# Splitting 24 weight pieces in the second half of the projection phase, and alternating two products in the tail

## The chip, the cores and the metric

One core of one Trainium2 chip. The metric is the device time of one execution in microseconds (us), the median of several runs.

## What is computed

One layer of a hybrid encoder on 2048 prompt and 32 sample tokens, model width 1024, all in float32. `z = rmsnorm(x) @ W_in` gives q, k, v, an attention gate, the inputs of a short convolution, and two merge gates. What matters here is what follows:

```python
y_a = (attn * silu(gate_a)) @ w_attn_out          # 512 -> 1024
y_c = (b_gate * conv * silu(gate_c)) @ w_conv_out # 512 -> 1024
r = x + (sigmoid(merge_a) * y_a + sigmoid(merge_c) * y_c) @ w_o
r = r + sigmoid(r @ w_ple_gate) * (p @ w_ple_proj)
```

## The kernel before

**Arithmetic.** A float32 product is made of three TensorE passes: each operand is split into a high half, rounded to the fast format fp32r, and a low half, the rest; the passes are high x high, high x low, low x high. ScalarE makes the high half with a copy, VectorE the low half with a subtraction (`split`, L228). A *piece*, or quad, is a weight tile of 128 x 512 numbers, 256 KB. The three large matrices W_in, W_o (`UO`) and W_pg (`UPG`) go through Strassen-Winograd: seven products instead of eight, for which four sums of weight pieces are needed (`make_sums` L353 for W_in, `quad_sums` L381 for W_o and W_pg: sc, a21, a11 and a12, four additions on VectorE). The sums are stored in DRAM by DMAs that GpSimd issues.

**Phases.** Tokens are worked on in two halves. The first phase (0 to about 870 us in the trace) is the projection with W_in: `steps` (L244 to L288), first the 21 groups of the first half `(0, g, p)`, then those of the second half `(1, g, p)`, whose products p = 2, 3, 4 are split once more into sets (`run_set`, L755; the letters A to G are its small products; GpSimd adds the weights for p = 3 and 4 in `load_set`, L448). A scheduler puts the instructions of this phase in order on each engine; a pool of 15 temporaries (`tp`, tag `t`, L50) serves the evictions, and from group 7 on `second_half` (L571), which loads rows of x, normalises them, combines them and stores them. The rest (yB, pp, yA, and the Strassen products with W_o and W_pg, called b0-50, b0-58, b1-50, b1-58 for the two halves) is a list of units, `plan` (L307 to L318), which `run_units` (L2020) issues in order; a planner in the kernel keeps a clock of its own (`now`, `busy`, `fin`), and decides by it when evictions, loads (`next_loads`, L1961) and the 17 attention tiles (`attention`, L1380; the start times stand in `begin`, L2070 to L2079) are issued between the products. All engines execute their queues in order.

**The 24 pieces.** The four sums of each of four columns of W_o make 16 pieces, the upper half of the yA/yB weights (`wa`) makes 8. They are wanted split in the second phase, so the kernel splits them in the first: at steps `(0, g, 6)` and `(0, g, 7)` of the first half, the loads at the first and the rest one step later (`sums_at`, L1234 to L1237). `quad_sums(UO, n)` runs at g = 1, 3, 5, 7, `piece_split(n)` (L394) at g = 2, 4, ... 16, `quad_sums(UPG, n)`, which stores unsplit sums, at g = 9, 11, 13, 15. The quads lie in a pool of their own (`zpool`, five buffers, L1232). `store_split` (L375) splits and stores both halves, 512 KB. In the second phase such a piece comes back as one load of 512 KB, straight into the split weights (`stored`, L399; L1998 to L2009); all other weights are loaded raw, 256 KB, and split there by ScalarE and VectorE (`split_w`, L1947).

**The planner's wire.** `Engine.call` (L141) reckons when a DMA has landed. In the second phase `wire[0]` is None after `restart()` (L211), so a transfer counts 5.2 us, one that accumulates 6.6 us, however many are under way.

**The tail of the first half.** `plan` has the 28 products of b0-58 (W_pg), then the eight units yA of block 2, then the first four products of b1-50.

## Time and profile before

| | us |
|---|---|
| median of 3 runs | 1543.53 |
| lowest and highest run | 1542.6, 1543.53 |
| the profiled execution | 1542.36 |
| its span, first to last instruction | 1540.6 |
| TensorE (PE) busy | 1501.9 |
| VectorE (DVE) busy | 1196.2 |
| ScalarE (ACT) busy | 795.0 |
| GpSimd (POOL) busy | 388.5 |

The profile is of one execution. PE is TensorE's matmul, PEld its loading of weights, SPq SyncE's queue of DMA issues. L158 is the line in the planner's helper from which nearly all instructions of the second phase come, so there one goes by tiles. In rows of stages the last three numbers are the granted clock of TensorE (1.00 is full), the busy share of the 16 DMA engines, and GB/s. "Busy" counts only instructions that compute; the time before an instruction is idle time, and the arrow names what ended it.

### The profile page before, as it was taken

The numbers are of one execution on the slowest core, as the hardware profiler recorded it, in microseconds if no ns is written. First come the engines' busy times: TensorE is split into PE (matmuls) and PEld (weight loads), VectorE is DVE, ScalarE is ACT, GpSimd is POOL, SyncE is SP. The second block draws the span as 40 slices with busy tenths as digits, with TensorE's granted clock in tenths as the row PEclk, the third lists the DMA queues.
The fourth block names the chain that finished last, engine by engine and source line by source line (L and its number), as shares of the span: only waits on it lengthen the run. The fifth ranks groups of instructions, "written<-read, shape, count | busy, mean of one in ns | idle before, by whom it ended". The sixth has DMA issues, their size and how long they took to land.

```text
span 1540.6 us, 27844 instructions
## 1 busy us (share of the span) xinstructions
PE 1501.9 (97%) x9553; PEld 1354.6 (88%) x9553; DVE 1196.2 (78%) x2290; ACT 795.0 (52%) x1893; POOL 388.5 (25%) x566
## 2 busy tenths in 40 slices
PE   9999999989999999999999999999999999899998
PEld 7778888768889999999999999998888788799998
DVE  7896887777568877799966778867898899367777
ACT  8364355234457654443445646685755668132453
POOL 2133332233221332333311221102313112110201
PEclk9999999999999999999999999999999999999999
DMA  9469798899887964334556785779888759998959
GB/s 362 161 224 358 263 326 270 294 334 348 287 281 249 319 218 155 123 118 133 158 182 195 249 257 184 216 251 255 252 238 244 193 153 262 325 300 267 278 147 286
DMA packets 202941, 374.14 MB, mean 243 GB/s; under 512 B 24368, under 2 KB 57712, under 8 KB 202800
## 3 DMA queue, kind: packets, MB, share of 16 engines
q1 hardware_dynamic: 158160, 258.30, 51.7%
q0 software_dynamic: 34992, 96.24, 21.2%
q10 hardware_dynamic: 9648, 17.83, 3.1%
q8 instruction: 75, 1.23, 0.3%
q14 instruction: 66, 0.54, 0.1%
HBM read 246.53 MB, written 125.85 MB: 242 GB/s over the span
## 4 chain that ended last, share of the span: by engine, by line
PE 72%; DMA 11%; DVE 7%; issue 6%; ACT 3%; POOL 1%; SPq 0%; POOLq 0%; DVEq 0%; ACTq 0%
PE b L158 13%; PE a L638 7%; PE a L643 7%; PE a L640 7%; PE yB L158 6%; PE la L776 5%; PE yA L158 4%; PE c L638 3%; PE c L640 3%; PE c L643 3%; DMA wr<-in_wu 3%; PE lc L776 2%; DVE c L158 2%; PE O L158 2%; PE S L158 1%
## 5 line engine op out<-in xcount | busy, mean ns | idle before, releaser
L158 PE MATMUL b<-xb_h,w 128*128 128x264 f32 (+1 forms) x1344 | 311.5, 324 | 0.0
L158 PEld LDWEIGHTS b<-xb_h,w 128*128 128x128 f32 x1344 | 223.6, 189 | 19.3 <-DVE c L158 1.4
L638 PE MATMUL a<-x_h,w 128*128 128x264 f32 (+1 forms) x744 | 228.7, 321 | 7.5 <-ACT u L832 6.1
L640 PE MATMUL a<-x_l,w 128*128 128x264 f32 (+1 forms) x744 | 228.5, 320 | 0.0
L158 PE MATMUL b<-xb_l,w 128*128 128x264 f32 (+1 forms) x672 | 218.4, 325 | 2.3 <-DVE xb_l L158 2.3
L643 PE MATMUL a<-x_h,w 128*128 128x264 f32 (+1 forms) x744 | 202.2, 321 | 0.0
L229 ACT CAST w<-wr 128x512 fp32r<-128x512 f32 (+1 forms) x180 | 110.0, 618 | 112.6 <-PE c L643 32.4
L230 DVE TENSOR_TENSOR w<-wr,w 128x512 fp32r<-128x512 f32 (+1 forms) x180 | 135.7, 764 | 39.7 <-ACT w L229 39.5
L638 PEld LDWEIGHTS a<-x_h,w 128*128 128x128 f32 x744 | 140.4, 189 | 19.2 <-ACT u L832 7.0
L640 PEld LDWEIGHTS a<-x_l,w 128*128 128x128 f32 x744 | 140.4, 189 | 10.7
L158 PEld LDWEIGHTS b<-xb_l,w 128*128 128x128 f32 x672 | 126.9, 189 | 12.4 <-DVE xb_l L158 3.8
L643 PEld LDWEIGHTS a<-x_h,w 128*128 128x128 f32 x744 | 125.3, 188 | 10.8 <-DVE w L230 0.2
L776 PE MATMUL la<-x_h,w 128*128 128x264 f32 x516 | 111.6, 285 | 1.0 <-ACT w L229 0.7
L158 ACT CAST w<-wr 128x512 fp32r<-128x512 f32 x104 | 63.7, 620 | 92.9 <-PE b L158 50.5
L638 PE MATMUL c<-x_h,w 128*128 128x512 f32 (+1 forms) x336 | 110.9, 340 | 0.0
L640 PE MATMUL c<-x_l,w 128*128 128x512 f32 (+1 forms) x336 | 110.8, 340 | 0.0
L643 PE MATMUL c<-x_h,w 128*128 128x512 f32 (+1 forms) x336 | 100.3, 340 | 0.0
L158 PE MATMUL yA<-ac_h,w 128*128 128x264 f32 (+1 forms) x384 | 93.6, 330 | 6.0 <-DMA w<-wa 5.9
L229 ACT CAST w<-a 128x512 fp32r<-128x512 f32 x82 | 49.0, 620 | 85.6 <-DVE a L360 48.8
L158 PE MATMUL yB<-ycs_h,w 128*128 128x264 f32 (+1 forms) x384 | 90.4, 325 | 0.0
L837 DVE SCALAR_TENSOR_TENSOR u<-u,c 128x264 f32<-128x264 f32 (+1 forms) x125 | 59.4, 506 | 39.8 <-ACT u L832 28.5
L776 PEld LDWEIGHTS la<-x_h,w 128*128 128x128 f32 x516 | 86.9, 188 | 1.6 <-ACT w L229 1.0
(446 smaller groups left out, 3861.9 us busy)
## 6 DMA issues: line engine op xcount, KB each, us to landing
wr<-in_wu SPq DMA_DIRECT2D x145, 256.0 KB, 4.5
a<-in_wu SPq DMA_DIRECT2D x116, 256.0 KB, 5.6
wr<-ws SPq DMA_DIRECT2D x74, 256.0 KB, 3.7
w<-wa SPq DMA_DIRECT2D x32, 512.0 KB, 5.7
w<-qs SPq DMA_DIRECT2D x32, 512.0 KB, 5.4
ws<-a POOLq DMA_DIRECT2D x63, 256.0 KB, 3.7
wr<-qs SPq DMA_DIRECT2D x32, 256.0 KB, 4.6
qs<-a POOLq DMA_DIRECT2D x24, 256.0 KB, 6.5
```

Source lines behind the costliest of these rows:

```text
L158: return f(**kw)
L229: nc.scalar.copy(out=hi, in_=src)
L230: nc.vector.tensor_tensor(out=lo, in0=src, in1=hi.bitcast(F32), op=sub)
L638: nc.tensor.matmul(out=ps[:, :cn], lhsT=w[:, 0, k], rhs=x[0][:, c0:c0 + cn], start=first and k == 0, stop=False, skip_group_check=True)
L640: nc.tensor.matmul(out=ps[:, :cn], lhsT=w[:, 0, k], rhs=x[1][:, c0:c0 + cn], start=False, stop=False, skip_group_check=True)
L643: nc.tensor.matmul(out=ps[:, :cn], lhsT=w[:, 1, k], rhs=x[0][:, c0:c0 + cn], start=False, stop=k == 3, skip_group_check=True)
L776: nc.tensor.matmul(out=ps[:, :m], lhsT=w[:, a, k], rhs=r[:, cols], start=q in "ABG" and j == 0 and e == 0, stop=j == 1 and e == 2, skip_gr ...
L837: nc.vector.scalar_tensor_tensor(out=t[:, c0:c0 + cn], in0=t[:, c0:c0 + cn], scalar=-1.0, in1=ps[:, :cn], op0=mul, op1=sub)
```

## The change

1. **Sums and splits apart.** `quad_sums` now only adds and stores the four sums unsplit, for W_o and W_pg alike, all eight calls in groups 1 to 8 of the first half, loads and additions in one step. Its quads and sum lie in the shared pool of 15 temporaries.
2. **Splits in the second half.** The 24 pieces are split by `half_steps`, in four stages with a distance: load (lag 0), ScalarE's copy (lag 9), VectorE's subtraction (lag 11), two stores (lag 12). The pieces follow one another at an even pitch over the steps from (1, 3, 1) on, by step lengths that the code assumes; `in_turn` fixes the place of each in its engine's queue. Their tiles use the pool of five buffers.
3. **Raw weights for the last yA.** `stored` gives split pieces for yA of blocks 0 and 1 only; blocks 2 and 3 load 256 KB and split.
4. **Alternation.** The eight yA units of block 2 alternate with the last eight products of b0-58.
5. **The planner.** `wire[0]` starts at 0.0 in the second phase, so DMAs queue for a shared wire (360 KB per us, 190 for accumulation). Attention tiles 8 to 16 begin 10 us earlier and a little closer together, and the gated attention rows of blocks 2 and 3 may be split earlier (`ac_open`).

```diff
+                        rate = 390e3 if not LATE["V"] else 360e3 if kw.get("accum_op") is None else 190e3
+                        wire[0] = end = max(end + 1.7, wire[0]) + o.shape[0] * size(o) * 4 / rate
...
-    plan += first[:4] + pps[12:] + mixed(1, first[4:8]) + first[8:] + products_of(0, UPG)
-    plan += [("yA", 2, n) for n in NA[2]] + second[:4] + mixed(3, second[4:8]) + second[8:] + products_of(1, UPG)
+    plan += first[:4] + pps[12:] + mixed(1, first[4:8]) + first[8:]
+    tail, ys = products_of(0, UPG), [("yA", 2, n) for n in NA[2]]
+    plan += tail[:-8] + [v for i in range(8) for v in (ys[i], tail[i - 8])]
+    plan += second[:4] + mixed(3, second[4:8]) + second[8:] + products_of(1, UPG)
...
     def quad_sums(x, n):
-        t = {name: quad_load(f"{name}_{x}_{n}", x + u, e)
-             for name, u, e in (("a11", n, 0), ("a21", n + 4, 0), ("a22", n + 4, 1), ("a12", n, 1))}
-        yield
-        t["sc"] = zp.tile([P, 4 * P], F32, tag="z", name=f"sc_{x}_{n}")
+        t = {}
+        for name, u, e in (("a11", n, 0), ("a21", n + 4, 0), ("a22", n + 4, 1), ("a12", n, 1)):
+            t[name] = tmp(f"{name}_{x}_{n}")[:, :512]
+            nc.sync.dma_start(out=t[name].rearrange("p (a b) -> p a b", a=4), in_=wu[x + u, :, 4 * e:4 * e + 4, :])
+        t["sc"] = tmp(f"sc_{x}_{n}")[:, :512]
...
         for p, o in ((7, "sc"), (5, "a21"), (6, "a11"), (3, "a12")):
-            if x == UO:
-                store_split(quad_sum[x, n][:, WS[p]], t[o], f"{p}_{x}_{n}")
+            nc.gpsimd.dma_start(out=quad_sum[x, n][:, WS[p]], in_=t[o])
+
+    def in_turn(engine):
+        return tc.issue_after(next(i for i in reversed(nc.cur_bb.bb.instructions) if i.engine == engine))
+
+    def half_steps(key, dst):
+        name = "_".join(map(str, key))
+        t = zp.tile([P, 4 * P], F32, tag="z", name=f"z{name}")
+        with in_turn(nc.sync.engine):
+            if key[0] == "wa":
+                nc.sync.dma_start(out=t.rearrange("p (a b) -> p a b", a=4), in_=wu[UY + key[1], :, 0:4, :])
             else:
-                nc.gpsimd.dma_start(out=quad_sum[x, n][:, WS[p], 0], in_=t[o])
+                nc.sync.dma_start(out=t, in_=quad_sum[UO, key[1]][:, WS[key[2]]])
+        yield
+        h = zp.tile([P, 4 * P], F32R, tag="z", name=f"h{name}")
+        with in_turn(nc.scalar.engine):
+            nc.scalar.copy(out=h, in_=t)
+        yield
+        with in_turn(nc.vector.engine):
+            nc.vector.tensor_tensor(out=t.bitcast(F32R), in0=t, in1=h.bitcast(F32), op=sub)
         yield
+        with in_turn(nc.gpsimd.engine):
+            nc.gpsimd.dma_start(out=dst[:, 0], in_=h.bitcast(F32))
+            nc.gpsimd.dma_start(out=dst[:, 1], in_=t)
+        yield

     def stored(key):
-        if key[0] == "q" and key[3] == 0:
-            return wa_split[key[2] - UY]
+        if key[0] == "q" and key[3] == 0 and key[1] < 2:
+            return halves["wa", key[2] - UY]
...
-    sums_at = {(0, 1 + 2 * n, 6): quad_sums(UO, n) for n in range(4)}
-    sums_at.update({(0, 9 + 2 * n, 6): quad_sums(UPG, n) for n in range(4)})
-    sums_at.update({(0, 2 + 2 * n, 6): piece_split(n) for n in range(8)})
-    sums_at.update({(0, g, 7): v for (_, g, _), v in sums_at.items()})
+    sums_at = {(0, 1 + 2 * n + e, 6): (x, n) for n in range(4) for e, x in enumerate((UO, UPG))}
+    length = [(2.9 if len(steps[i][0]) == 3 else 0.75) if i >= at_step[1, 3, 1] else 0.0 for i in range(len(steps))]
+    pitch = (sum(length) - 24) / len(halves)
+    half_at = sorted((pitch * j + lag, j, k) for j in range(len(halves)) for k, lag in enumerate((0, 9, 11, 12)))
...
+        while half_at and length[i] and half_at[0][0] <= sum(length[:i]):
+            next(half_gen[half_at.pop(0)[1]])
...
     LATE.update(V=0.08, S=0.1, G=0.25)
+    wire[0] = 0.0
...
-        t = (0, 6)[e] if e < 2 else 11 * e if e < 8 else e1 - 30 + (e2 - e1) * (e - 8) / 9
+        t = (0, 6)[e] if e < 2 else 11 * e if e < 8 else e1 - 40 + 0.96 * (e2 - e1) * (e - 8) / 9
...
-    begin.append((T[f"b0{UPG}_0_2"], lambda: ac_open.add(2)))
-    begin.append((T[f"b1{UO}_0_2"], lambda: ac_open.add(3)))
+    begin.append((T[f"b0{UPG}_0_5"], lambda: ac_open.add(2)))
+    begin.append((T[f"b0{UPG}_1_4"], lambda: ac_open.add(3)))
```

The scheduler of the first phase orders each queue anew. SyncE's queue where the first rows of x for the second half (b00 to b11) are loaded, near 265 us in the trace; wr and a are weights of the current groups, wa_5 a piece of yA, a11_58 to a22_58 quads of W_pg's sums. Before:

```order
L348 DMA wr87_2783<-in_wu 128x512
L372 DMA wa_5_2873<-in_wu 128x512
L372 DMA a11_58_2_3064<-in_wu 128x512
L372 DMA a21_58_2_3066<-in_wu 128x512
L583 DMA b00_0_2801<-in_xT 128x528
L583 DMA b01_0_2804<-in_xT 128x528
L583 DMA b10_0_2807<-in_xT 128x528
L583 DMA b11_0_2810<-in_xT 128x528
L372 DMA a22_58_2_3068<-in_wu 128x512
L348 DMA wr88_2836<-in_wu 128x512
```

The same place on SyncE's queue after the change:

```order
L351 DMA wr87_2743<-in_wu 128x512
L593 DMA b00_0_2761<-in_xT 128x528
L593 DMA b01_0_2764<-in_xT 128x528
L593 DMA b10_0_2767<-in_xT 128x528
L593 DMA b11_0_2770<-in_xT 128x528
L351 DMA wr88_2787<-in_wu 128x512
```

Four piece loads that stood between the two weights wr87 and wr88 have left this place. All quad loads of the eight sums now stand ahead of the last load of group 9's sums, among the loads of groups 3 to 9.

The tail, on SyncE's queue, where the weights of yA of block 2 are loaded (w or wr with a number is a weight, tk2 the merge gate of a yA unit, pp and out_yT belong to products of W_pg). Before:

```order
L158 DMA w445_15986<-wa0_145 128x1024
L158 DMA out_yT<-c21_058_0_7_15128 128x512
L158 DMA out_yT<-c21_058_1_7_15157 128x512
L158 DMA z_at_79<-at3_3_15668 512x1x128
L158 DMA tk2_7_16028<-z_t0_7_107 128x528
L158 DMA w446_16035<-wa1_146 128x1024
L158 DMA tk2_0_16061<-z_t0_0_100 128x528
L158 DMA out_yT<-c21_058_2_7_15204 128x512
L158 DMA w447_16069<-wa2_147 128x1024
L158 DMA tk2_1_16095<-z_t0_1_101 128x528
```

The weights in the tail after the change:

```order
L159 DMA wr445_15924<-in_wu 128x512
L159 DMA out_yT<-c22_058_3_5_15790 128x512
L159 DMA tk2_6_15935<-z_t0_6_106 128x528
L159 DMA wr446_15949<-in_wu 128x512
L159 DMA pp0_2_15973<-z_pp2_86 128x512
L159 DMA wr447_15975<-in_wu 128x512
L159 DMA out_yT<-c12_058_2_6_15235 128x512
L159 DMA tk2_7_15996<-z_t0_7_107 128x528
L159 DMA wr448_15998<-in_wu 128x512
```

Loads of 1024 numbers per row have become loads of 512, and loads of pp for W_pg's products stand between the tk2 loads. On TensorE attention's last product (O_31) stands just ahead of the first yA unit of block 2 in both orders; eight products of b0-58 that stood before it now stand behind it. Its tile 8 (pq2_0) has moved from the fifth unit of yA of block 0 to the second.

More of the change, by code (lines that the diff above doesn't have):

```diff
@@ L155, in call @@
                         o = kw["out"]
-                        wire[0] = end = max(end + 1.7, wire[0]) + o.shape[0] * size(o) * 4 / 390e3
+                        rate = 390e3 if not LATE["V"] else 360e3 if kw.get("accum_op") is None else 190e3
+                        wire[0] = end = max(end + 1.7, wire[0]) + o.shape[0] * size(o) * 4 / rate
                 fin[0] = max(fin[0], end)
@@ L364, in make_sums @@
             nc.gpsimd.dma_start(out=wsum[g][:, i], in_=sums[g][p])
-    quad_sum = {(x, n): dram.tile([P, 4, 1 + (x == UO), 4 * P], F32, tag=f"qs{x}_{n}", name=f"qs{x}_{n}")
-                for x in (UO, UPG) for n in range(4)}
-    wa_split = [dram.tile([P, 2, 4 * P], F32, tag=f"wa{n}", name=f"wa{n}") for n in range(8)]
-    def quad_load(name, u, e):
-        t = zp.tile([P, 4 * P], F32, tag="z", name=name)
-        nc.sync.dma_start(out=t.rearrange("p (a b) -> p a b", a=4), in_=wu[u, :, 4 * e:4 * e + 4, :])
-        return t
-    def store_split(dst, t, name):
-        h = tmp(f"h{name}", F32R)[:, :512]
-        split(h, t.bitcast(F32R), t)
-        nc.gpsimd.dma_start(out=dst[:, 0], in_=h.bitcast(F32))
-        nc.gpsimd.dma_start(out=dst[:, 1], in_=t)
-    def quad_sums(x, n):
-        t = {name: quad_load(f"{name}_{x}_{n}", x + u, e)
-             for name, u, e in (("a11", n, 0), ("a21", n + 4, 0), ("a22", n + 4, 1), ("a12", n, 1))}
-        yield
-        t["sc"] = zp.tile([P, 4 * P], F32, tag="z", name=f"sc_{x}_{n}")
+    quad_sum = {(x, n): dram.tile([P, 4, 4 * P], F32, tag=f"qs{x}_{n}", name=f"qs{x}_{n}") for x in (UO, UPG) for n in range(4)}
+    halves = {("wa", n): dram.tile([P, 2, 4 * P], F32, tag=f"wa{n}", name=f"wa{n}") for n in range(8)}
+    halves.update({("o", n, p): dram.tile([P, 2, 4 * P], F32, tag=f"o{n}_{p}", name=f"o{n}_{p}")
+                   for n in range(4) for p in WS})
+    def quad_sums(x, n):
+        t = {}
[3 more added lines that the diff above has]
+        t["sc"] = tmp(f"sc_{x}_{n}")[:, :512]
         for o, v, w in (("sc", "a11", "a21"), ("a21", "a21", "a22"), ("a11", "a11", "a21"), ("a12", "a12", "a11")):
@@ L388, in quad_sums @@
         for p, o in ((7, "sc"), (5, "a21"), (6, "a11"), (3, "a12")):
[L389 to L395 removed]
+            nc.gpsimd.dma_start(out=quad_sum[x, n][:, WS[p]], in_=t[o])
[7 more added lines that the diff above has]
+                nc.sync.dma_start(out=t.rearrange("p (a b) -> p a b", a=4), in_=wu[UY + key[1], :, 0:4, :])
+            else:
+                nc.sync.dma_start(out=t, in_=quad_sum[UO, key[1]][:, WS[key[2]]])
         yield
[L397 removed]
+        h = zp.tile([P, 4 * P], F32R, tag="z", name=f"h{name}")
[9 more added lines that the diff above has]
+        yield
     def stored(key):
[L400 to L401 removed]
+        if key[0] == "q" and key[3] == 0 and key[1] < 2:
+            return halves["wa", key[2] - UY]
         if key[0] == "B" and key[2] == UO and key[4] in WS:
[L403 removed]
+            return halves["o", key[3], key[4]]
         return None
@@ L1233, in tile_hybrid_stream_step @@
     zp = zpool.__enter__()
-    sums_at = {(0, 1 + 2 * n, 6): quad_sums(UO, n) for n in range(4)}
-    sums_at.update({(0, 9 + 2 * n, 6): quad_sums(UPG, n) for n in range(4)})
-    sums_at.update({(0, 2 + 2 * n, 6): piece_split(n) for n in range(8)})
-    sums_at.update({(0, g, 7): v for (_, g, _), v in sums_at.items()})
+    sums_at = {(0, 1 + 2 * n + e, 6): (x, n) for n in range(4) for e, x in enumerate((UO, UPG))}
+    length = [(2.9 if len(steps[i][0]) == 3 else 0.75) if i >= at_step[1, 3, 1] else 0.0 for i in range(len(steps))]
+    pitch = (sum(length) - 24) / len(halves)
+    half_at = sorted((pitch * j + lag, j, k) for j in range(len(halves)) for k, lag in enumerate((0, 9, 11, 12)))
+    half_gen = [half_steps(*x) for x in halves.items()]
     conv_at = {(1, G - 1, 1): lambda: conv_load(0), (1, G - 1, 6): lambda: (conv_split(0), conv_load(1)),
@@ L1252, in tile_hybrid_stream_step @@
         if todo[0] in sums_at:
-            next(sums_at[todo[0]], None)
+            quad_sums(*sums_at[todo[0]])
+        while half_at and length[i] and half_at[0][0] <= sum(length[:i]):
+            next(half_gen[half_at.pop(0)[1]])
         if i in after:
@@ L1993, in next_loads @@
             else:
-                eY.dma_start(out=t, in_=quad_sum[key[2:4]][:, WS[key[4]], 0].rearrange("p (a b) -> p a b", a=4))
+                eY.dma_start(out=t, in_=quad_sum[key[2:4]][:, WS[key[4]]].rearrange("p (a b) -> p a b", a=4))
             raw_of[i] = t
```

4 lines of the change are left out of this document (removed).

## The prediction

> **What bounds the kernel now.** I read the first page for the share of each engine, then busy time by stage (which stage leaves TensorE idle, and what is full there), then TensorE in order of time for the single stops, and last the queues that end those stops.
>
> From the page: the span and the busy time of each engine.
>
> ```profile
> span 1540.6 us, 27844 instructions
> PE 1501.9 (97%) x9553; PEld 1354.6 (88%) x9553; DVE 1196.2 (78%) x2290; ACT 795.0 (52%) x1893; POOL 388.5 (25%) x566
> ```
>
> TensorE is busy for 1501.9 of 1540.6 us, and the change removes no product. So it can win only the 38.7 us of idle time and what the clock loses behind a stop. Busy time by stage (PE, PEld, DVE, ACT, POOL; then granted clock, DMA share, GB/s) shows where that lies:
>
> ```profile
> 100.00:275.00 175.00, 175.00 (x758) 141.42 (x757) 139.52 (x229) 82.79 (x168) 63.19 (x120) 1.00 0.86 306
> 275.00:345.00 70.00, 58.77 (x233) 46.05 (x232) 51.88 (x83) 20.32 (x36) 23.36 (x44) 0.93 0.89 313
> 642.00:774.00 132.00, 132.00 (x1086) 131.81 (x1085) 122.50 (x244) 56.57 (x123) 50.09 (x71) 1.00 0.44 135
> 1070.00:1310.00 240.00, 234.59 (x1250) 195.96 (x1249) 214.33 (x425) 164.17 (x477) 61.73 (x64) 0.99 0.82 227
> 1195.00:1220.00 25.00, 21.60 (x101) 16.80 (x100) 23.43 (x46) 13.85 (x40) 6.71 (x7) 0.93 0.95 244
> 1310.00:1350.00 40.00, 33.55 (x244) 32.30 (x243) 15.83 (x34) 7.20 (x14) 6.94 (x8) 0.91 1.08 330
> ```
>
> Three stretches leave TensorE idle: 11.2 us in 275 to 345, 3.4 us in 1195 to 1220, 6.45 us in 1310 to 1350. In the last two the DMA engines are full (0.95 and 1.08), in the first nearly (0.89). In the second half of the first phase (642 to 774) TensorE never waits, DMA is at 0.44, and VectorE is at 122.5 of 132 us, that is 93%. TensorE's stops one by one (start, duration, then in brackets the idle time ahead and what ended it):
>
> ```profile
> 283.40 0.80 PE L638 MATMUL b<-x_h,w 128*128 128x512 f32 x1 [3.75 <-ACT w L229]
> ...
> 313.64 0.50 PE L638 MATMUL a<-x_h,w 128*128 128x512 f32 x1 [2.46 <-ACT u L832]
> ...
> 324.10 0.50 PE L638 MATMUL a<-x_h,w 128*128 128x512 f32 x1 [1.36 <-ACT s L832]
> ...
> 338.71 0.50 PE L638 MATMUL a<-x_h,w 128*128 128x512 f32 x1 [3.66 <-ACT u L832]
> ...
> 1202.83 0.66 PE L158 MATMUL pq<-cst,zq 128*128 128x128 f32 x4 [2.04 <-DMA zq<-z_q]
> ...
> 1331.84 0.56 PE L158 MATMUL yA<-ac_h,w 128*128 128x264 f32 x1 [4.80 <-DMA w<-wa]
> ```
>
> Behind a long stop the clock is low for some microseconds, which costs again. The same columns in short stages:
>
> ```profile
> 280.00:285.00 5.00, 1.60 (x4) 1.20 (x5) 4.78 (x8) 2.27 (x5) 2.81 (x6) 0.69 1.05 404
> 285.00:290.00 5.00, 5.00 (x16) 3.98 (x15) 4.32 (x7) 0.86 (x2) 2.08 (x5) 0.62 1.00 361
> 310.00:315.00 5.00, 2.54 (x12) 1.74 (x11) 5.00 (x10) 2.14 (x4) 4.13 (x8) 1.00 0.95 357
> 340.00:345.00 5.00, 5.00 (x16) 3.95 (x15) 1.80 (x4) 2.22 (x4) 0.54 (x1) 0.66 1.03 371
> 1200.00:1205.00 5.00, 2.96 (x14) 2.19 (x13) 4.20 (x7) 0.86 (x3) 2.40 (x3) 0.85 1.10 304
> 1205.00:1210.00 5.00, 5.00 (x20) 3.92 (x19) 4.90 (x9) 1.96 (x7) 2.85 (x3) 0.81 1.04 299
> 1330.00:1335.00 5.00, 3.16 (x14) 3.20 (x15) 0.52 (x3) 0.64 (x1) 0.86 (x1) 0.50 1.07 385
> 1335.00:1340.00 5.00, 5.00 (x37) 5.00 (x36) 3.55 (x8) 1.27 (x2) 1.74 (x2) 0.83 1.06 358
> ```
>
> I price the low clock as busy time times what is missing to 1.00. After the 3.75 us stop: 1.60 x 0.31 + 5.00 x 0.38 = 2.4 us. After the 3.66 us stop: 5.00 x 0.34 = 1.7. After the 2.04 us stop: 2.96 x 0.15 + 5.00 x 0.19 = 1.4. After the 4.80 us stop: 3.16 x 0.50 + 5.00 x 0.17 = 2.4. So the stretches are worth 11.2 + 4.1 = 15.3 us, 3.4 + 1.4 = 4.8 us and 6.45 + 2.4 = 8.9 us, 29 us in all.
>
> The Trainium skill (TensorE: Matmul & The Clock Gate, What's actually happening) says that an idle window of about 3.4 us halves the clock. The stops of 3.75, 3.66 and 4.80 us agree, and 2.46 us at 311 kept its clock; but 2.04 us at 1201 did lose it, so the measurement decides. By the rule that stretch would be 3.4 us and not 4.8, and the sum below would not change.
>
> **The change, part by part.**
>
> *Pieces leave the first half.* The stop at 279.7 is made by the pieces directly. SyncE's queue, in order, then VectorE behind the late x rows:
>
> ```profile
> 266.28 5.16 SPq L372 DMA_DIRECT2D a<-in_wu  x2
> 271.53 2.42 SPq L583 DMA_DIRECT2D b<-in_xT  x4
> 274.06 0.36 SPq L372 DMA_DIRECT2D a<-in_wu  x1
> 274.53 0.67 SPq L348 DMA_DIRECT2D wr<-in_wu  x1
> ```
>
> ```profile
> 329.62 1.45 DVE L544 SCALAR_TENSOR_TENSOR b<-b,cst,rb 128x528 f32<-128x528 f32 x2 [1.53 <-DMA b<-in_xT]
> ...
> 333.06 0.77 DVE L544 SCALAR_TENSOR_TENSOR b<-b,cst,rb 128x528 f32<-128x528 f32 x1 [1.38 <-DMA b<-in_xT]
> ```
>
> Two piece loads (L372) held SyncE for 5.16 us, and the weights wr, which ScalarE and then TensorE need, were issued only at 274.53. In the changed order no piece load stands behind the a9 loads, so this stop and its clock go: 3.75 + 2.4 = 6.15 us. The stop at 335 follows from late x rows: VectorE waits 1.53 and 1.38 us for them in order, and the four sums and the weight halves queue behind it. The transfers that made them late are those of the UPG sums and of the wa pieces, all earlier or later now: 3.66 + 1.7 = 5.4 us, which I count as gone. The stops of 2.46 and 1.36 us have VectorE full (5.00 of 5 us), and only a few of its instructions there belong to pieces; I count half, 1.9 us. Sum: 13.4 us. What is next there are VectorE's own rows, busy 51.9 of 70 us.
>
> Against that, all 32 sums now run in groups 1 to 8. By order, 32 quad loads instead of 20 stand ahead of a9's end; with the stores it is 64 transfers of 256 KB instead of about 60, since a sum is stored once and not as two halves; DMA was at 0.86 there without one stop. But the sums now take five of the 15 temporaries that evictions and second_half use, not a pool of their own, and SyncE stops in order when none is free. No trace shows that; it costs nothing if one is always free, and 6.15 us for each stop of the kind above. I take half a stop, 3 us. First half: -13.4 + 3 = -10.4 us.
>
> *The splits go to the second half.* The durations, from groups of instructions in the first half and, for the first row, in 640 to 760:
>
> ```profile
> L230 DVE TENSOR_TENSOR w<-wr,w 128x512 fp32r<-128x512 f32 x42 | 31.6, 766 | 0.0
> L230 DVE TENSOR_TENSOR a<-a,h 128x512 fp32r<-128x512 f32 x12 | 7.7, 684 | 0.0
> L229 ACT CAST h<-a 128x512 fp32r<-128x512 f32 x12 | 7.0, 619 | 2.4 <-DVE a L387 2.3
> L378 POOL DMA_DIRECT2D qs<-h x16 | 8.6, 540 | 6.1 <-ACT h L229 5.8 <-issue 0.4
> ```
>
> How long the stage is, from the chain of waits (start, duration; lc is the last product of a set, yB opens the next phase):
>
> ```profile
> 801.95 1.46 PE lc L776 x12
> ...
> 835.55 1.46 PE lc L776 x12
> ...
> 876.63 4.42 PE yB L158 x19
> ```
>
> Each of 24 pieces brings one load, 0.62 us of ScalarE, 0.68 to 0.77 us of VectorE and two GpSimd issues of 0.54 us. They are spread evenly from step (1, 3, 1) on. From there to 876 are nearly nine and a half sets of 33.6 us, 318 us, less 24 at the end: one piece every 12.25 us. In 642 to 774 that is 11 pieces: VectorE 122.5 + 11 x 0.766 = 130.9 of 132 us, ScalarE 56.6 + 6.8, GpSimd 50.1 + 11.9. DMA gets 24 x 768 KB in 294 us, 64 GB/s on 135. Everything hides as long as VectorE stays below full; locally it will lag by a microsecond or two, which prefetched weights and the eight banks cover. Queued behind a piece's subtraction are VectorE's weight halves, for which TensorE waits next. If that cover is gone, the price is what exceeds the stage. I take +1 us, bounds 0 and +6.
>
> The Trainium skill (GPSIMD Engine Reference, the table of specifications) has GpSimd and VectorE sharing their SBUF interface, with contention for instructions that read two SBUF inputs, as the subtraction does; that speaks against putting splits beside GpSimd's sums. The trace agrees in size: 766 ns beside them against 684. By the rule it is 24 x 0.08 = 2 us more of VectorE, which the figure of 130.9 already holds.
>
> *Raw weights for the last two yA blocks, and the alternation.* DMA from 1270 to 1360:
>
> ```profile
> DMA packets 14372, 27.54 MB, mean 306 GB/s; under 512 B 1478, under 2 KB 3014, under 8 KB 14362
> ...
> w<-wa SPq DMA_DIRECT2D x13, 512.0 KB, 7.9
> ```
>
> These 13 loads halve: 13 x 262 KB = 3.4 MB of 27.5, or 11 us of a full queue. The stop of 4.80 us waits for exactly such a load, and in the new order a yA weight is due every second product and not every one. I take 6.5 of the 8.9 us as gone. The 16 splits added (about 0.62 us of ScalarE and 0.69 of VectorE each, as above) fall where VectorE is busy 15.8 of 40 us; I take +0.5, at worst one late weight of 3 us.
>
> *Attention closer together.* A product is 12 matmuls at 175.00 / 758 = 0.231 us, 2.8 us. By order, eight products now stand between attention's end and the same place as before, and it begins three units earlier: it ends some 22 us earlier and begins some 8 us earlier, 14 us shorter. VectorE has 240 - 214.3 = 25.7 us free in 1070 to 1310, so the same work needs about 214 of 226 us, 95%. That makes small waits likelier; the planner's wire model, which now knows that transfers queue, makes the 2.04 us wait for zq less likely. I set the two against each other: 0, bounds -4.8 and +5.
>
> Sum: -10.4 + 1 - 6.5 + 0.5 + 0 = -15.4 us. The profiled execution took 1542.4 us (its span and 1.8 around it), 1.2 under the median of the runs, 1543.5. So 1527.0 for such an execution, 1528 for a median. By the bounds, 1519 to 1537.
>
> **The rivals.**
>
> 1. Everything goes, and nothing new comes: all 29 us, so 1514.5. For it: all three stretches have a full queue, and all of them lose transfers. Against it: the 2.46 us stop with a full VectorE. Chance 0.12.
> 2. Only the first half gains. The last stage stays at a full queue, since 24 of its 27.5 MB remain, and the stop moves to another load; denser attention adds 3 us: -10.4 + 1 + 3 = -6.4, so 1537. Chance 0.13.
> 3. The change does not do what it says: the pieces' transfers only move from 205 to 345 into 100 to 205, where DMA is at 0.86 already. Two stops of 6.15 us come there, the last stage gains half of its 6.5: -13.4 + 12.3 - 3.3 + 1.5 = -3, taken as no change, 1541 to 1545. Chance 0.08.
> 4. Slower: the temporaries. Each of the eight sums takes five of 15; from group 7 on second_half takes nine for a row of x. If SyncE then stops in front of a quad load, the weights behind it are late as at 266. It decides from the fourth such stop on (20 us of gain against 6.15 each); with five of eight, -13.4 + 30.7 - 6.5 + 1 = +12, so 1555. For it: SyncE did stop for 5.16 us on a full pool. Against it: from 100 to 275 piece loads stood in its queue too, and TensorE never waited. Chance 0.12.
>
> **How the numbers follow.** The forecast has 0.55. A measurement of this kernel can tell about 0.2% (3 us) from no change. Faster by more: the forecast, rivals 1 and 2, 0.80; within: rival 3, 0.08; slower: rival 4, 0.12. The range reaches from rival 1 to the edge of rival 3, 1514 to 1541; outside are rival 4 and about half of rival 3. The forecast's own range is 1519 to 1537.
>
> **What would show it.** Right: no stop over 3 us between 275 and 345 and the clock at 1.00 there; TensorE still busy in all of 642 to 774 with VectorE at 97% or more; in the last alternating products no stop over 3 us, and no load of 512 KB from wa there. Wrong: SyncE waiting several microseconds ahead of a quad load before 205 with TensorE stopped behind it (rival 4); TensorE idle in 540 to 840 (the splits are not hidden); the clock low anywhere between 1270 and 1350 (rival 2).

## The result and the profile after

The changed kernel takes 1522.5 us (median of 4 runs, 1520.8 to 1524.9) against 1543.1 us before (4 runs, 1540.4 to 1543.5). The ratio is 0.9871, with a 95% interval of 0.9853 to 0.9890. That is 20.6 us less, where the forecast had 15.4 less (1528, range 1514 to 1541). The profiled execution took 1524.9 us, 1523.1 of them span.

From the page of the changed kernel, the span and the busy time of each engine:

```profile
span 1523.1 us, 28003 instructions
PE 1496.8 (98%) x9553; PEld 1353.3 (89%) x9553; DVE 1211.4 (80%) x2306; ACT 802.5 (53%) x1909; POOL 392.5 (26%) x582
```

TensorE's idle time fell from 38.7 to 26.3 us. Busy time by stage of the changed kernel, in the columns used before (stretch, its length, then PE, PEld, DVE, ACT and POOL; granted clock, DMA share, GB/s):

```profile
100.00:275.00 175.00, 175.00 (x758) 141.29 (x757) 139.28 (x226) 72.30 (x148) 57.33 (x106) 1.00 0.84 297
275.00:345.00 70.00, 70.00 (x303) 56.53 (x302) 57.49 (x91) 25.62 (x44) 23.44 (x44) 1.00 0.88 308
642.00:774.00 132.00, 127.72 (x1029) 125.67 (x1028) 120.58 (x248) 61.30 (x132) 50.48 (x84) 1.00 0.63 201
1070.00:1310.00 240.00, 232.91 (x1299) 199.95 (x1298) 205.30 (x408) 154.96 (x440) 58.52 (x62) 0.99 0.82 227
1310.00:1350.00 40.00, 40.00 (x287) 37.90 (x286) 29.18 (x52) 18.95 (x37) 8.60 (x10) 1.00 1.05 325
```

In 275 to 345 TensorE is busy all the time and does 303 matmuls where it did 233. In 1310 to 1350 it is busy all the time at full clock, though DMA is still full. But in 642 to 774, where it never waited before, it now does 1029 matmuls in place of 1086. VectorE is busy for only 120.6 of those 132 us.

The cleanest view of the whole is three stages, marked by two products that open a new stage: the first la (the sets of the second half begin) and the first yB. What follows the first yB, the kernel's second phase with attention, W_o and W_pg, is called the third phase from here on, since the two halves before it count as two stages. These are TensorE's rows in order of time, of the kernel before and then of the changed one:

```profile
460.26 0.28 PE L776 MATMUL la<-x_h,w 128*128 128x264 f32 x1
...
874.53 0.39 PE L158 MATMUL yB<-ycs_h,w 128*128 128x512 f32 x1
```

```profile
443.15 0.28 PE L786 MATMUL la<-x_h,w 128*128 128x264 f32 x1
...
866.54 0.40 PE L159 MATMUL yB<-ycs_h,w 128*128 128x512 f32 x1
```

The first stage became 17.1 us shorter (460.3 to 443.2). The second became 9.1 us *longer* (414.3 to 423.4). The third became 9.5 us shorter (666.1 to 656.6, up to the end of the span). The same three numbers, read in the same way from each run, carry the experiments:

| kernel | to la | la to yB | yB to end | ratio to before (95%) |
|---|---|---|---|---|
| before | 460.3 | 414.3 | 666.1 | 1 |
| after | 443.2 | 423.4 | 656.6 | 0.9871 (0.9853 to 0.9890) |
| e1: third phase put back | 441.1 | 421.8 | 666.6 | 0.9936 (0.9923 to 0.9949) |
| e2: old estimate and starts | 441.7 | 421.7 | 664.8 | 0.9941 (0.9924 to 0.9957) |
| e3: raw weights, no alternation | 439.5 | 423.0 | 667.0 | 0.9951 (0.9936 to 0.9967) |
| e4: alternation, no raw weights | 443.3 | 421.9 | 663.6 | 0.9936 (0.9922 to 0.9949) |
| e5: subtractions left out | 441.2 | 417.2 | 656.8 | 0.9832 (0.9815 to 0.9848) |
| e6: stages at other places | 441.3 | 416.2 | 656.3 | 0.9828 (0.9810 to 0.9846) |
| e7: subtractions on GpSimd | 441.1 | 422.7 | 656.5 | 0.9893 (0.9874 to 0.9911) |
| e8: old attention starts | 439.9 | 422.8 | 664.0 | 0.9930 (0.9907 to 0.9953) |
| e9: old estimate, new starts | 441.2 | 421.9 | 661.5 | 0.9889 (0.9872 to 0.9906) |
| e10: sums in five shared tiles | 448.8 | 422.2 | 656.7 | 0.9921 (0.9906 to 0.9935) |
| e11: e6 with all yA weights raw | 441.2 | 415.8 | 665.0 | 0.9886 (0.9870 to 0.9902) |
| e12: e6 with two small moves | 441.1 | 415.4 | 664.8 | 0.9853 (0.9836 to 0.9869) |

The stages are those of one profiled execution of each kernel, the ratios are of all runs. For the changed kernel and for e12 the profiled execution was the slowest of four (1524.9 us with a median of 1522.5, and 1523.0 with 1518.8), so their stages together are some us too long; for e2 and e7 it was a fast one (1529.9 with 1532.0, and 1522.1 with 1525.1).

Kernels with the same first half differ by up to 3.8 us in the first column (439.5 to 443.3). Where nothing in it was changed the second column repeats within 1.7 us (421.7 to 423.4) and the third within 0.5 (656.3 to 656.8 in five kernels). The changed kernel's 423.4 is the top of its range: the mean of the eight kernels with this second half is 422.3, which is 8.0 us above the kernel before.

### The profile page after: what moved, and what is told of

Read it like the earlier page. It is cut to its first block, busy times and chain, and to the rows that moved or that the text cites. A ratio compares the mean times of both kernels' runs of the same rounds, so it can differ in the third digit from the quotient of the medians.

```text
span 1523.1 us, 28003 instructions
## 1 busy us (share of the span) xinstructions
PE 1496.8 (98%) x9553; PEld 1353.3 (89%) x9553; DVE 1211.4 (80%) x2306; ACT 802.5 (53%) x1909; POOL 392.5 (26%) x582
## 4 chain that ended last, share of the span: by engine, by line
PE 80%; DVE 8%; DMA 4%; issue 3%; ACT 3%; POOL 2%; SPq 0%; DVEq 0%; ACTq 0%; POOLq 0%
PE b L159 17%; PE a L653 6%; PE a L648 6%; PE a L650 6%; PE yA L159 6%; PE yB L159 5%; PE la L786 4%; PE c L648 3%; PE c L653 3%; PE c L650 3%; PE pp L159 3%; PE lc L786 2%; PE O L159 2%; PE S L159 2%; DVE w L231 1%
## 5 line engine op out<-in xcount | busy, mean ns | idle before, releaser
L648 PE MATMUL a<-x_h,w 128*128 128x264 f32 (+1 forms) x744 | 227.3, 320 | 0.0
L653 PE MATMUL a<-x_h,w 128*128 128x264 f32 (+1 forms) x744 | 198.7, 320 | 0.9 <-DVE w L231 0.9
L231 DVE TENSOR_TENSOR w<-wr,w 128x512 fp32r<-128x512 f32 (+1 forms) x180 | 142.3, 801 | 26.7 <-ACT w L230 24.9
L648 PEld LDWEIGHTS a<-x_h,w 128*128 128x128 f32 x744 | 140.0, 188 | 10.6
L159 PEld LDWEIGHTS b<-xb_l,w 128*128 128x128 f32 x672 | 126.5, 188 | 10.6 <-DVE xb_l L159 2.0
L159 ACT CAST w<-wr 128x512 fp32r<-128x512 f32 x120 | 74.0, 620 | 88.3 <-PE b L159 47.4
L159 DVE TENSOR_TENSOR w<-wr,w 128x512 fp32r<-128x512 f32 x120 | 82.7, 695 | 20.4 <-ACT w L159 20.0
L847 DVE SCALAR_TENSOR_TENSOR u<-u,c 128x264 f32<-128x264 f32 (+1 forms) x125 | 59.4, 508 | 43.2 <-ACT u L842 28.7
```

What stands on the lines that cost most here:

```text
L159: return f(**kw)
L231: nc.vector.tensor_tensor(out=lo, in0=src, in1=hi.bitcast(F32), op=sub)
L648: nc.tensor.matmul(out=ps[:, :cn], lhsT=w[:, 0, k], rhs=x[0][:, c0:c0 + cn], start=first and k == 0, stop=False, skip_group_check=True)
L653: nc.tensor.matmul(out=ps[:, :cn], lhsT=w[:, 1, k], rhs=x[0][:, c0:c0 + cn], start=False, stop=k == 3, skip_group_check=True)
L847: nc.vector.scalar_tensor_tensor(out=t[:, c0:c0 + cn], in0=t[:, c0:c0 + cn], scalar=-1.0, in1=ps[:, :cn], op0=mul, op1=sub)
```

## The experiments

My theory after the result: the first half gains by the pieces' leaving it, the tail by fewer bytes, each by its own edit, and the second half gives 9 us back because 24 subtractions stand in VectorE's queue.

### The third phase: which of its edits made the gain

**e1** puts the third phase back as it was and leaves the sums and the moved splits:

```diff
-    plan += tail[:-8] + [v for i in range(8) for v in (ys[i], tail[i - 8])]
+    plan += tail + ys
```

```diff
-        if key[0] == "q" and key[3] == 0 and key[1] < 2:
+        if key[0] == "q" and key[3] == 0:
```

```diff
-                        rate = 390e3 if not LATE["V"] else 360e3 if kw.get("accum_op") is None else 190e3
+                        rate = 390e3
...
-    wire[0] = 0.0
```

```diff
-        t = (0, 6)[e] if e < 2 else 11 * e if e < 8 else e1 - 40 + 0.96 * (e2 - e1) * (e - 8) / 9
+        t = (0, 6)[e] if e < 2 else 11 * e if e < 8 else e1 - 30 + (e2 - e1) * (e - 8) / 9
```

```diff
-    begin.append((T[f"b0{UPG}_0_5"], lambda: ac_open.add(2)))
-    begin.append((T[f"b0{UPG}_1_4"], lambda: ac_open.add(3)))
+    begin.append((T[f"b0{UPG}_0_2"], lambda: ac_open.add(2)))
+    begin.append((T[f"b1{UO}_0_2"], lambda: ac_open.add(3)))
```

In this order: alternation, raw weights, transfer estimate, starts of attention, and the products at which the rows of blocks 2 and 3 are let in.

> The new kernel with its third phase put back: plan without alternation, all yA weights read as stored halves, the planner's old transfer estimate, the old starts of attention. What is left of the change are the merged sums and the 24 pieces split in the second half. Theory (the gain is made in the first half and in the tail, each by its own edit; the second half gives some 9 us back): the sets begin some 17 us earlier, yB some 8 us earlier, and the tail's stop of 6 us between 1310 and 1350 is there again; 1535 us, 1532 to 1538. Rival (the tail runs without a stop because the pieces have moved, and not because of the raw weights): no stop over 3 us in the tail, 1524 to 1528.

Measured: 1531.1 us (1530.4 to 1533.0). The third phase takes 666.6 us, as before the change (666.1). The stop in the tail is there again. TensorE's rows in e1:

```profile
1308.61 0.36 PE L159 MATMUL yA<-ac_h,w 128*128 128x264 f32 x1 [1.41 <-DMA w<-wa]
...
1319.83 0.56 PE L159 MATMUL yA<-ac_h,w 128*128 128x264 f32 x1 [4.77 <-DMA w<-wa]
```

It came out 1 us under the range, since its first two stages are 2.1 and 1.6 us shorter than the changed kernel's. So the rival is out: moving the pieces does nothing for the tail. All 9.5 us of the third phase belong to the third phase's own edits. (The last of them, the products that let rows in, was put back only here, together with the others, so its own share is not known.)

**e2** takes back the third and the fourth of these diffs alone, estimate and starts.

> The new kernel with the planner's old transfer estimate and the old starts of attention; raw weights and alternation stay. Theory (the third phase's gain is the raw weights'; the planner's edit moves little): 1522 to 1526, and the stop of 4.6 us at a z_q load near 1099 is gone or elsewhere. Rival (the planner's model of the transfers makes the gain of the third phase, about 9 us): 1529 to 1534 with stops over 3 us after 1190.

Measured: 1532.0 us (1529.7 to 1535.2), a third phase of 664.8 us. My theory failed here. The tail's stop is gone, yet nearly nothing is gained. Who waited in TensorE between 1030 and 1400 in e2 (total us, times, longest):

```profile
PE b L159 <- DVE c L159: 4.3, 1, 4.3
PE b L159 <- ACT xb_h L159: 3.6, 1, 3.6
PE pq L159 <- DMA zq<-z_q: 3.1, 2, 2.4
```

These are products (b) and scores (pq) that wait for VectorE and ScalarE and for z_q, a row of attention's q loaded from DRAM. The time that the tail won is lost ahead of it.

**e3** undoes only the alternation (the first diff), **e4** only the raw weights (the second).

> The new kernel without the alternation: yA of block 2 stands again behind the last W_pg products; raw weights stay. Theory (fewer bytes end the tail's stop): 1522 to 1526, no stop over 3 us between 1310 and 1350. Rival (spacing the 512 KB loads does it): 1527 to 1532, with a stop of 3 to 7 us there.

> The new kernel with the alternation, but the yA weights of blocks 2 and 3 read again as stored halves of 512 KB. Theory (bytes): a stop of 2 to 6 us on w<-wa between 1310 and 1360, 1526 to 1531. Rival (spacing): no stop over 2 us there, 1521 to 1524.

Measured: e3 1533.8 us (1531.1 to 1535.3), e4 1531.2 us (1530.3 to 1533.5). Neither edit gains the whole without the other. e3 has the stop that its rival named, at 1533.8 us somewhat above the rival's range, and e4 has the stop on w that its theory named, 0.2 us above the theory's range; so neither bytes alone nor spacing alone explains the tail. TensorE's rows in the tail of e3, then of e4:

```profile
1326.22 0.39 PE L159 MATMUL b<-xb_l,w 128*128 128x264 f32 x1 [1.34 <-DVE xb_l L159]
1330.92 0.59 PE L159 MATMUL b<-xb_l,w 128*128 128x264 f32 x1 [4.07 <-DVE xb_l L159]
1335.03 0.59 PE L159 MATMUL b<-xb_l,w 128*128 128x264 f32 x1 [3.08 <-DVE xb_l L159]
```

```profile
1301.94 0.39 PE L159 MATMUL yA<-ac_h,w 128*128 128x264 f32 x1 [3.58 <-DMA w<-wa]
...
1317.30 0.36 PE L159 MATMUL yA<-ac_h,w 128*128 128x264 f32 x1 [2.16 <-DMA w<-wa]
```

With raw weights in a block of eight, no yA product waits for its weight any more, but the rows behind are late. VectorE in order of time in e3:

```profile
1328.69 0.77 DVE L159 SCALAR_TENSOR_TENSOR tk<-tk,yA 128x264 f32<-128x264 f32 x2 [1.92 <-DMA tk<-z_t]
```

VectorE waits there 1.92 us for a tk row from DRAM, and the product at 1330.92 waits for the halves (xb_l) made of it. Less than half of its 4.07 us is that row: VectorE still has three instructions to do behind it (0.77, 0.71 and 0.70 us), and without the alternation no other product stands between the last yA and these. So halving the weights ends the wait for a weight and brings the chain of the next unit to light. Alternating with weights of 512 KB only cuts the stop in parts. With both, no product waits in 1310 to 1350, though the DMA engines are as full as before (1.05 against 1.08); that each late load then has a product of W_pg ahead of it would explain this, but no run shows it by itself.

**e8** takes back the starts alone (the fourth diff), **e9** the estimate alone (the third). e9 was made after e8, with a theory changed by it.

> The new kernel with the planner's new transfer estimate but the old starts of attention (30 us ahead of yA, full spacing). Theory (the transfer estimate is what places loads early enough, the starts are small): 1521 to 1526, and the stop of 4.6 us on a z_q load near 1099 moves. Rival (the earlier and closer starts carry the gain that was lost with the old planner): 1528 to 1533, with stops over 3 us between 1120 and 1260.

> The new kernel with the planner's old transfer estimate alone; the new starts of attention (40 us ahead of yA, 0.96 of the spacing) stay, as do raw weights and alternation. Theory, formed after the run with the old starts lost 7 us: the starts carry that gain by themselves, so this kernel runs as the new one does, 1521 to 1525. Rival (estimate and starts only work together): 1528 to 1533, with stops over 3 us between 1120 and 1260.

Measured: e8 1529.5 us (1528.0 to 1538.3), third phase 664.0; e9 1525.7 us (1524.1 to 1526.4), third phase 661.5. By the stages the starts are worth 7.4 us beside the new estimate (664.0 to 656.6) and 3.3 us beside the old one (664.8 to 661.5). The estimate is worth 4.9 us beside the new starts. So in e8 my first theory fell, the starts are not small, though the rival's sign, a stop of over 3 us, is missing too: e8's longest in the third phase is 2.54 us. In e9 the theory "starts alone" fell as well: the time is 0.7 us above its range, and the third phase loses 4.9 us. In e9 two single stops remain, one of 4.8 us (b on xb_l) and one of 2.8 us (b on w).

### The second half: where 9 us went

In 642 to 774 of the changed kernel TensorE stops about once in every 34 us, the period of the sets. TensorE in order of time:

```profile
653.95 0.39 PE L786 MATMUL la<-x_h,w 128*128 128x264 f32 x1 [0.81 <-DVE u L802]
...
655.59 0.39 PE L786 MATMUL lc<-x_h,w 128*128 128x264 f32 x1 [0.17 <-DVE o L802]
```

And VectorE in order of time ahead of it, where L402 is the subtraction of a piece, L231 the halves of weights, and L802 and L847 the evictions that free TensorE's banks:

```profile
648.34 0.77 DVE L847 SCALAR_TENSOR_TENSOR u<-u,c 128x264 f32<-128x264 f32 x2
649.02 0.69 DVE L402 TENSOR_TENSOR zwa<-zwa,hwa 128x512 fp32r<-128x512 f32 x1
649.62 1.29 DVE L231 TENSOR_TENSOR w<-wr,w 128x512 fp32r<-128x512 f32 x2
650.82 0.77 DVE L847 SCALAR_TENSOR_TENSOR u<-u,c 128x264 f32<-128x264 f32 x2
...
653.46 0.43 DVE L802 TENSOR_TENSOR u<-u,la 128x264 f32<-128x264 f32 x1
```

VectorE has no gap here, from 640.6 to 659.7: it serves a full queue in order. The eviction of la at 653.46 frees the bank for the matmul at 653.95, and 0.69 us of a piece stand in the queue ahead of it. Idle time is not all of the price. From the first la to yB TensorE is idle for 7.9 us in place of 2.0, and it is busy for 415.5 us in place of 412.2, for the same matmuls at a granted clock of 1.00. These 3.3 us, too, lie around the stops (28 matmuls in 3.83 us of 654 to 658, where 4.00 us have 35 elsewhere); what they are was not taken apart.

**e5** leaves the subtraction out, so that the low halves are stored unsplit and the products that read them are not the reference's.

```diff
-        with in_turn(nc.vector.engine):
-            nc.vector.tensor_tensor(out=t.bitcast(F32R), in0=t, in1=h.bitcast(F32), op=sub)
```

> The new kernel without VectorE's subtraction in the 24 split stages, so that the stored low halves are the unsplit piece and the products that read them are wrong; loads, ScalarE copies and stores stay. The second half took 414.3 us from its first la to the first yB product before, and 423.4 us after. Theory (24 subtractions of 0.7 us stand between evictions in VectorE's bursts): 414 to 417 us for that stretch, 1514 to 1517 in all. Rival (the pieces' transfers, or the stores that GpSimd issues, slow the half): still 421 to 424 us, 1521 to 1524.

**e6** keeps all 24 stages and puts them elsewhere, away from the sets of the convolution's groups:

```diff
-    length = [(2.9 if len(steps[i][0]) == 3 else 0.75) if i >= at_step[1, 3, 1] else 0.0 for i in range(len(steps))]
-    pitch = (sum(length) - 24) / len(halves)
-    half_at = sorted((pitch * j + lag, j, k) for j in range(len(halves)) for k, lag in enumerate((0, 9, 11, 12)))
+    length = [(2.9 if len(steps[i][0]) == 3 else 0.75) if i >= at_step[1, 0, 1] else 0.0 for i in range(len(steps))]
+    start = [7.8 * j if j < 14 else 243.0 + 8.0 * (j - 14) for j in range(len(halves))]
+    half_at = sorted((start[j] + lag, j, k) for j in range(len(halves)) for k, lag in enumerate((0, 9, 11, 12)))
```

> The new kernel with the same 24 stages at other places: 14 pieces at a pitch of 7.8 in some 515 to 625 us and 10 at a pitch of 8 in 765 to 840 us, none of them in the convolution's groups between 640 and 760 where VectorE is full. Theory (the place is what costs, not the number): 415 to 418 us from the first la to yB, 1514 to 1518 in all. Rival (any added 16 us of VectorE in a half whose VectorE is 80 to 90 per cent busy costs about half of itself): 421 to 424 us, 1521 to 1524.

**e7** does the subtraction on GpSimd:

```diff
-        with in_turn(nc.vector.engine):
-            nc.vector.tensor_tensor(out=t.bitcast(F32R), in0=t, in1=h.bitcast(F32), op=sub)
+        with in_turn(nc.gpsimd.engine):
+            nc.gpsimd.tensor_tensor(out=t.bitcast(F32R), in0=t, in1=h.bitcast(F32), op=sub)
```

> The new kernel with the stages' subtraction on GpSimd in place of VectorE. Theory (VectorE's queue is what costs): most of the loss goes, 416 to 419 us from la to yB, less what VectorE is slowed beside a GpSimd operation; 1516 to 1519 in all. Rival (the slowing beside GpSimd costs as much as the subtraction): 421 to 425 us, 1521 to 1526.

Measured: e5 1515.9 us (1515.2 to 1517.0), e6 1515.6 us (1513.1 to 1517.5), e7 1525.1 us (1522.1 to 1529.7). The second stage took 417.2, 416.2 and 422.7 us. Without its 24 subtractions it is 6.2 us shorter, with every load, ScalarE copy and store still there: what is left over before, 2.9 us, is all that these may cost. With all the work at other places it is 7.2 us shorter: the place costs, not the number. (Against the mean of 422.3 these are 5.1 and 6.1 us.) In e5 the stretch of 642 to 774:

```profile
642.00:774.00 132.00, 131.32 (x1077) 130.90 (x1076) 116.87 (x236) 63.50 (x135) 57.42 (x92) 1.00 0.69 220
```

In e6 the stretch of the new pieces, and the same one, which now has two of its eleven subtractions:

```profile
525.00:540.00 15.00, 12.71 (x100) 12.08 (x99) 14.94 (x28) 9.02 (x20) 5.20 (x10) 1.00 0.93 314
642.00:774.00 132.00, 132.00 (x1083) 131.60 (x1082) 118.78 (x242) 59.95 (x129) 47.15 (x68) 1.00 0.52 161
```

VectorE is hardly less busy in 642 to 774 than in the changed kernel (118.8 against 120.6 us), yet TensorE doesn't wait. Nine of the eleven subtractions left it (the other two stand behind 764), and the rest of its queue moved up. What is left of the price now stands at 525 to 540, where the first pieces make VectorE full (14.94 of 15 us). e6 beats both kernels.

GpSimd is no way out. Between 545 and 860 in e7, the subtraction there, and VectorE's halves beside it (count, total us, mean ns, then idle time before):

```profile
L402 POOL TENSOR_TENSOR zo<-zo,ho 128x512 fp32r<-128x512 f32 x16 | 22.6, 1411 | 35.2 <-ACT ho L399 35.1
...
L231 DVE TENSOR_TENSOR w<-wb,w 128x512 fp32r<-128x512 f32 x17 | 15.8, 932 | 0.0
```

In the changed kernel that second group takes 684 ns each. GpSimd needs 1411 ns where VectorE needs some 700, and this group of VectorE's gets longer by a third. Not every group does: the largest, w<-wr, has 837 ns against 862 in the changed kernel. But over the whole second stage VectorE is busy for 346.0 us in e7, 349.1 in the changed kernel and 335.4 in e5, which has no such subtraction. So of the 13.7 us that the subtractions cost VectorE, 10.6 are still there, and the rival holds (422.7 in its range of 421 to 425). The Trainium skill (GPSIMD Engine Reference, 4.1 Engine selection) puts two-input elementwise work on GpSimd at about twice VectorE's time; the trace agrees.

### The first half: buffers or splits

**e10** takes the tiles of the quad sums from the pool of five, in place of temporaries:

```diff
-            t[name] = tmp(f"{name}_{x}_{n}")[:, :512]
+            t[name] = zp.tile([P, 4 * P], F32, tag="z", name=f"{name}_{x}_{n}")
-        t["sc"] = tmp(f"sc_{x}_{n}")[:, :512]
+        t["sc"] = zp.tile([P, 4 * P], F32, tag="z", name=f"sc_{x}_{n}")
```

> The new kernel with the quad sums' loads and sums in the five shared tiles that before used, in place of temporaries; the splits stay out of the first half. Theory (SyncE stood behind loads that waited for a tile): SyncE waits for stores again ahead of the quad loads and a part of the stops between 100 and 345 is back, first la at 446 to 455, 1526 to 1534. Rival (the splits' own time on ScalarE, VectorE and in the stores made the first half late): first la at 439 to 444 as with the new kernel, 1521 to 1525.

Measured: 1530.2 us (1529.4 to 1530.5), first la at 448.8. The numbers fit my theory, but the place does not. Busy time by stage in e10:

```profile
0.00:100.00 100.00, 93.25 (x378) 72.55 (x379) 82.81 (x139) 59.04 (x108) 26.60 (x53) 0.97 0.84 298
100.00:275.00 175.00, 175.00 (x756) 140.87 (x755) 134.33 (x215) 72.11 (x148) 49.09 (x91) 1.00 0.72 252
275.00:345.00 70.00, 70.00 (x302) 56.48 (x301) 57.75 (x91) 25.59 (x44) 22.45 (x44) 1.00 0.87 304
```

No stop between 100 and 345 came back. All of the loss lies in the first 100 us, where the changed kernel has TensorE busy for 96.49. The tiles are free from the start, so the sums' loads and sums go there at once. VectorE's sums (L381) in 0 to 100, in e10 and then in the changed kernel:

```profile
L381 DVE TENSOR_TENSOR a<-a,a 128x512 f32<-128x512 f32 x11 | 7.5, 685 | 0.1
L381 DVE TENSOR_TENSOR sc<-a,a 128x512 f32<-128x512 f32 x4 | 2.8, 690 | 0.6 <-DMA a<-in_wu 0.5
```

```profile
L381 DVE TENSOR_TENSOR sc<-a,a 128x512 f32<-128x512 f32 x1 | 0.7, 687 | 0.0
L381 DVE TENSOR_TENSOR a<-a,a 128x512 f32<-128x512 f32 x1 | 0.7, 686 | 0.0
```

Fifteen sums instead of two stand in VectorE's queue while it makes the first rows; the first quad load of e10 is issued at 26.6 us, that of the changed kernel at 89.9. TensorE's new stops there wait for rows made by VectorE and ScalarE, but the DMA share rose too (0.84 against 0.67), and the two were not taken apart. So the temporaries help the startup by keeping the sums out of it. The stops at 280 and 335 stay away without them as well. What else left that stretch are the pieces' loads, the splits and the doubled stores; that these made the stops is argued from the rows of the kernel before, and no run puts one of the three back.

### Two attempts at more

**e11** is e6 with all 32 yA weights raw. The eight wa pieces are neither split ahead nor stored:

```diff
-    halves = {("wa", n): dram.tile([P, 2, 4 * P], F32, tag=f"wa{n}", name=f"wa{n}") for n in range(8)}
-    halves.update({("o", n, p): dram.tile([P, 2, 4 * P], F32, tag=f"o{n}_{p}", name=f"o{n}_{p}")
+    halves = dict({("o", n, p): dram.tile([P, 2, 4 * P], F32, tag=f"o{n}_{p}", name=f"o{n}_{p}")
...
-        if key[0] == "q" and key[3] == 0 and key[1] < 2:
-            return halves["wa", key[2] - UY]
...
-    start = [7.8 * j if j < 14 else 243.0 + 8.0 * (j - 14) for j in range(len(halves))]
+    start = [20.0 + 9.0 * j if j < 10 else 243.0 + 8.0 * (j - 10) for j in range(len(halves))]
```

> The kernel with the stages at other places, and all 32 yA weights loaded raw: the eight pieces of W_yA are neither split ahead nor stored, which leaves 16 pieces, ten at a pitch of 9 in some 530 to 620 us and six at a pitch of 8 from 765. Theory (bytes: the z_q load behind two 512 KB loads lands late near 1090): that stop of 3.7 us and its clock go, 1509 to 1514. Rival (VectorE, 85 per cent busy in attention, now splits 16 more weights there): new stops on xb_l, w or PT between 1070 and 1310, 1516 to 1522.

Measured: 1524.2 us (1523.5 to 1527.2), 2 us above the rival's range. TensorE still waits twice for z_q, 1.5 and 1.8 us, where e6 has one stop of 3.7 us. The third phase takes 665.0 us, 8.7 more than in e6, with less to transfer. The rival was right that new stops take the place of the old one, here on attention's chain (PT waits for P four times, 2.4 us in all; O for ptl, 1.9 us; O for tb, 1.4 us). 5.4 us of TensorE's busy time are missing between 860 and 1070 (201.67 against 207.04 in e6), a stretch that was not foreseen.

**e12** is e6 with the first 14 pieces 20 us later at a pitch of 6.8, and attention's starts 44 us ahead in place of 40:

```diff
-    start = [7.8 * j if j < 14 else 243.0 + 8.0 * (j - 14) for j in range(len(halves))]
+    start = [20.0 + 6.8 * j if j < 14 else 243.0 + 8.0 * (j - 14) for j in range(len(halves))]
...
-        t = (0, 6)[e] if e < 2 else 11 * e if e < 8 else e1 - 40 + 0.96 * (e2 - e1) * (e - 8) / 9
+        t = (0, 6)[e] if e < 2 else 11 * e if e < 8 else e1 - 44 + 0.96 * (e2 - e1) * (e - 8) / 9
```

> The kernel with the stages at other places, with two changes that lie 500 us apart: the first 14 pieces start 20 us later at a pitch of 6.8, to end the stop of 2.3 us on VectorE between 525 and 540, and attention starts 44 us ahead of yA in place of 40, to issue the z_q load near 1081 some 4 us earlier. Theory (both stops are local, each goes with its own cause): no stop over 0.5 us between 515 and 640, the z_q stop near 1090 under 1.5 us at full clock, 1509 to 1513. Rival (attention's start is a finely set compromise, and moving it opens a stop elsewhere): the first stop goes all the same, but the third phase takes 2 to 8 us longer than with 40, 1515 to 1522.

Measured: 1518.8 us (1517.8 to 1523.0). The rival was right in kind: the third phase of the profiled execution is 8.5 us longer, where the rival had 2 to 8, and by the medians the whole kernel is 3.2 us slower than e6. In e12 the stretch from the second stage, and the new stop:

```profile
510.00:642.00 132.00, 132.00 (x1085) 131.81 (x1084) 103.40 (x197) 66.19 (x143) 57.15 (x88) 1.00 0.77 261
1115.00:1130.00 15.00, 11.29 (x41) 8.63 (x40) 13.56 (x25) 6.50 (x15) 5.07 (x5) 0.77 0.79 213
```

TensorE never waits in 510 to 642, and the stage is the shortest of all (415.4). The z_q stop near 1090 went as well (3.70 us in e6). But a stop of 3.4 us on xb_l at 1120 came with its low clock, and further ones behind it, and the third phase became longer than e6's by those 8.5 us in that execution. e6's third phase with e12's pieces should be some 1 us better than e6; that was not run.

## Why the prediction was right, and which of its steps were not

The likeliest case and the range held: the first half and the tail lose their long stops, and the sum is a gain of over 1%. Term by term, forecast against measured:

- **First half, -10.4 against -17.1 (mis-sized).** The stops and the low clock of 275 to 345, priced at 15.3 us, went altogether, where I had 13.4: I had counted only half of the two shorter stops, 2.46 and 1.36 us. The +3 for temporaries did not come and had the wrong sign, since e10 shows that they keep 6 to 8 us out of the startup. The rest, 1.8 us, is the startup's and within its spread.
- **Splits in the second half, +1 with bounds 0 and +6, against +9.1, or +8.0 by the mean of eight kernels (wrong, outside its bounds).** The step that failed is "everything hides as long as VectorE stays below full; locally it will lag by a microsecond or two, which prefetched weights and the eight banks cover". I had summed VectorE over 132 us, 130.9 of them busy. It was busy for 120.6 and TensorE waited all the same, since in each set VectorE has stretches without a gap, and there 0.7 us more are 0.7 us late. The sign named for this, TensorE idle in 540 to 840, is what the profile showed. A mean load of under 100% was no cover; e5 shows that the subtraction itself makes most of the loss, and e6 that the +1 was nearly to be had (+1.9) at other places. The transfers, which I had checked, are no cause of the larger part (e5).
- **Raw weights and alternation, -6.5 + 0.5.** The stop at 1331.84 and its clock, 8.9 us, went whole. My reason, 11 us of bytes, is not sufficient: e3 has the same bytes and a stop of 4 us behind another chain. The sentence on the alternation ("a yA weight is due every second product") was the necessary other half.
- **Attention closer together, 0 with bounds -4.8 and +5 (wrong size, a wrong reason).** The whole third phase is 9.5 us shorter, and without the new starts (e8) or without starts and estimate (e2) 7.4 and 8.2 us of that are lost. I had treated it as an addition beside the tail. The runs show that tail and attention are not two terms: each of e2, e3, e4 and e8 leaves the third phase within 2.5 us of before. A stop that goes in one place brings the next wait to light, and only the edits together bring the whole: taken back one at a time, alternation, raw weights, starts and estimate cost 10.4, 7.0, 7.4 and 4.9 us, more in sum than the 9.5 that they gain. The z_q stop that I expected to become less likely came back at another place. TensorE's row in the changed kernel, and then the busy time in two short stretches with the granted clock behind it:

```profile
1099.37 1.09 PE L159 MATMUL pq<-cst,zq 128*128 128x128 f32 x4 [4.61 <-DMA zq<-z_q]
```

```profile
1095.00:1100.00 5.00, 0.64 (x3) 0.67 (x4) 1.38 (x2) 0.00 (x0) 0.00 (x0) 0.84 1.09 327
1100.00:1105.00 5.00, 5.00 (x23) 4.71 (x22) 3.22 (x5) 3.17 (x11) 2.96 (x3) 0.50 0.89 245
```

Priced as in the prediction, wait and clock are 4.6 + 2.6 us, the largest single loss that the changed kernel has left.

Of the rivals, 1 (everything goes, nothing new comes) described the first half and the tail. Its condition, nothing new, failed in the second half; e6 with 1515.6 us is almost its 1514.5. Rival 2 had the right mechanism for e3, the stop moving elsewhere, and not for the change. Rivals 3 and 4 did not occur: no stop in 100 to 275.

The errors had opposite signs: -6.7 us in the first stage, +8.1 in the second, -3.5 in the third (-9.5 where the terms gave -6.0). That they nearly cancel is luck, and the total was nearer than its terms. It missed the span of the profiled execution by 2.1 us; the median lies another 2.4 us under that execution.

## What to carry to other kernels

An engine that serves a queue in order is a cover only where it has gaps: look at its load over the length of one burst, and put extra work into the light part of each period, which here was worth 7 us for the same 24 instructions. When a stop at the end of a full queue goes, ask which transfer or chain is next late, and test edits together and with one left out, because here leaving out one lost from half to all of what they gained together. A schedule's start times that were tuned with one set of loads are part of that set: moving them by 4 us of 1500 went with a kernel some 3 us slower.
